# A two-layer streaming encoder step: first tokens scaled before their transpose, step weights loaded once, fixed places for long-lived tiles

## The chip, the cores and the metric

One core of a Trainium2 chip runs the whole step as one program. The metric is device time in microseconds (us), from the profiler's clock; lower is better. Engines: PE is TensorE (its weight loads are listed as PEld), DVE is VectorE, ACT is ScalarE, POOL is GpSimd, SP is SyncE, which here issues every DMA. Each engine takes its instructions in the order that was fixed when the program was built.

## What is computed

Two request groups go through the same weights: a prompt of 1024 tokens and a sample of 32 tokens with carried states. Layer 0 is a Mamba-2 SSD mixer, layer 1 an HGRN2 mixer, each followed by a SwiGLU FFN. The parts that the change touches are the first norm, the input projections of the SSD mixer and the step `dt`:

```python
def rmsnorm(x, w):
    y = x * rsqrt(mean(x * x, -1) + 1e-6)
    return y * w
# SSD mixer, on h = rmsnorm(x, ssd_norm_w)
proj = h @ in_w                       # 1024 -> 5152 = z 2048, xbc 3072, dt 32
xbc  = silu(causal_conv4(proj[xbc]))  # x 2048, B 512, C 512
dt   = softplus(proj[dt] + dt_bias)
y, S = ssd_scan(x, dt, -exp(A_log), B, C, S0)
out  = (rmsnorm_groups((y + D * x) * silu(z)) * gnorm_w) @ out_w
# every layer: x = x + out;  x = x + (silu(hn @ w_gate) * (hn @ w_up)) @ w_down
```

## The kernel before, in words

Tokens come in two halves: half 0 is prompt tokens 0 to 511, half 1 is prompt tokens 512 to 1023 with the 32 sample tokens behind them (`LEN` 512 and 544). All activations are kept transposed, features on the partitions and tokens along the free dimension; the residual is `acc[h][m]`, eight tiles of 128 features per half. Every product is made of three matmuls of rounded halves: high by high, high by low, low by high (`product`, lines 282 to 284); so each normalized activation tile `h`, `l` and each weight tile `wh`, `wl` is a pair, made by a ScalarE copy and a VectorE subtraction (`split`, `wsplit`).

The opening (lines 1167 to 1179 and 576 to 590) does this:

- `x_rows` loads 128 tokens as two row tiles of 512 columns; `load_x` transposes them on TensorE (line 161), squares them on ScalarE with a running sum (`xss`), and copies the transposed pieces into `acc` (line 168 and ScalarE in turn).
- `x_norm` takes 256 tokens: `x_rstd` makes the reciprocal root of each token on POOL (`xr`, one column a chunk), `over_partitions` spreads it over all partitions by `diag` and a product with ones (lines 181, 182), and `norm` makes, for each of eight feature tiles, `xf = acc * w * rstd` on VectorE (line 330), `h` on ScalarE and `l` on VectorE.
- `first_vectors`, `head_vectors` and `other_vectors` load small vectors. `head_vectors` loads `dcol` from `ssd_D` in two DMAs whose elements lie two apart in memory.
- `ssd_layer` first makes conv tile 16, the step (`ssd_dt`), conv tile 20, then `load_x` for all five chunks of half 1, the later vectors, and conv tiles 0 to 3. For these first conv tiles and for the step of half 0 the tokens go in two blocks of 256 columns; everything else of half 0 uses 512. `ssd_dt` loads its 32 weight columns four times side by side, so that the result stands on all four groups of 32 partitions.

Then the units of the SSD mixer follow: four z tiles, the chunks of the scan, the gate and the output product, with the next unit's conv tiles between; then the FFN, the HGRN2 mixer and its FFN. In the FFN, `ffn_unit` makes 256 columns of gate or up by a seven-product scheme from `unit_weights`; `unit_raw` takes its raw weights by a counter `NU`: odd units use the big `Y` tile, even ones two of the three `raw` tiles. Up and gate units alternate, and the down products of a group (`ffn_outs`, four loads into `raw`) run right after the next group's first gate unit.

Buffers are named by tags with a fixed count (`BUFS`): `x` 12, `n` 4, `s` 5, `xn` 16 for the normalized pairs, `raw` 3, `ws` 6. Places and the order of instructions on every queue come from a planner (`TileContext(nc, auto_bufs=True)`), which puts tiles into memory by their lifetimes and lets a tile wait for the one whose bytes it takes over; `high_priority` lifts the norm by 600 places.

Of the kernel before, what the change touches and what calls it, by code (L numbers as in the profile page):

```python
# [16 lines left out]
P = 128  # L17
# [13 lines left out]
NG = 4  # L31
# [11 lines left out]
BUFS = {"xn": 16, "x": 12, "ys": 8, "cb": 4, "xd": 2, "ec": 1, "ss": 1, "xr": 2, "n": 4, "w": 3, "s": 5}  # L43
WIDTH = {k: 512 if k == "xr" else TW if k in ("x", "w") else LEN[1] for k in BUFS}


@with_exitstack
def trunk_kernel(ctx, tc, x_prompt, x_sample, state_ssd, cache_conv, state_hgrn,
# [23 lines left out]
    def small(s, w=P, dt=F32):  # L72
        return sp.tile([P, w], dt, tag="s", bufs=BUFS["s"], name=nm(s))

# [41 lines left out]
    ident = cp.tile([P, P], F32, name="ident")  # L116
    make_identity(nc, ident)
    ones = cp.tile([P, P], F32, name="ones")
    V.memset(ones, 1.0)
    epsc = cp.tile([P, 1], F32, name="epsc")  # L120
    V.memset(epsc, EPS)
    lss = cp.tile([P, 13], F32, name="lss")
    epst = lss[:, 12:13]
    mhalf = cp.tile([P, 8], F32, name="mhalf")
    G.memset(mhalf, -0.5)
    cmask = cp.tile([P, P], F32, name="cmask")
# [4 lines left out]
    rmask = cp.tile([P, LEN[1]], F32, name="rmask")  # L131
# [4 lines left out]
    for i in range(2):  # L136
        t = cp.tile([P, P], F32, name=f"scz{i}")
        V.memset(t, 0.0)
        scz.append(t)


    acc = [[cp.tile([P, LEN[h]], F32, name=f"acc{h}_{m}") for m in range(KD)] for h in range(2)]

    xss = cp.tile([P, 2, 9], F32, name="xss")
    xr = cp.tile([P, 9], F32, name="xr")
# [38 lines left out]
    vc = cp.tile([P, NVC], F32, name="vc")  # L184
    cw = cp.tile([P, 96], F32, name="cw")
    cc = cp.tile([P, 72], F32, name="cc")
    dtb = cp.tile([P, 1], F32, name="dtb")
    acol = cp.tile([P, 1], F32, name="acol")
    dcol = cp.tile([P, 16], F32, name="dcol")
    lbt = cp.tile([P, 6, 8], F32, name="lbt")  # L190
# [29 lines left out]
    def other_vectors():  # L220
        rows = T("n", "rows")[:, :P]
        for c, src in ((C_FFN, ffn_norm_w), (C_HGN, hgrn_norm_w), (C_GN, ssd_gnorm_w),
                       (C_HG, hgrn_gnorm_w), (C_LB, hgrn_lower_bounds)):
            n = src.shape[0] * src.shape[1] // P
            dma(rows[c - NV0:c - NV0 + n, :], src.rearrange("o (m p) -> (o m) p", p=P))
        columns(rows, NVC - NV0, vc[:, NV0:])
        V.tensor_scalar_mul(vc[:, C_GN:C_HG + 1], vc[:, C_GN:C_HG + 1], 0.5)
        rows = T("n", "rows")[:, :P]
        dma(rows[:72, :], cache_conv.rearrange("o b k (m p) -> (o b k m) p", p=P))
        columns(rows, 72, cc)  # L230
# [29 lines left out]
    def wraw(parts, kt):  # L260
        raw = wp.tile([P, 1024], F32, tag="raw", bufs=3, name=nm("raw"))
# [6 lines left out]
    def wsplit(raw, kt):  # L268
        wh = wp.tile([P, 1024], F32R, tag="ws", bufs=6, name=nm("wh"))
        wl = wp.tile([P, 1024], F32R, tag="ws", bufs=6, name=nm("wl"))  # L270
# [51 lines left out]
    def norm(h, wc, out, tags, blocks=None, r=None):  # L322

        for (b0, bn) in blocks or ((0, LEN[h]),):
# [3 lines left out]
            for m in range(KD):  # L328
                xf = T("n", "xf")
                stt(xf[:, :bn], acc[h][m][:, b0:b0 + bn], vc[:, wc + m:wc + m + 1], r[:, :bn], MUL, MUL)  # L330
                if m == len(out):
                    out.append((T(tags[2 * m], "h", F32R), T(tags[2 * m + 1], "l", F32R)))
# [10 lines left out]
    carry = cp.tile([P, NCT, 3], F32, name="carry")  # L343
    newc = cp.tile([P, 2, 3, NCT], F32, name="newc")
    Sst = [cp.tile([P, 512], F32, tag="st", bufs=NG, name=f"Sst{g}") for g in range(NG)]
    cumd = [dp.tile([32, LEN[h]], F32, name=f"cumd{h}") for h in range(2)]
    ecumd = [dp.tile([32, LEN[h]], F32, name=f"ecumd{h}") for h in range(2)]
    lastd = [dp.tile([32, 5], F32, name=f"lastd{h}") for h in range(2)]

    @lifted("dt")  # L350
    def ssd_dt(h, xn, blocks):
# [3 lines left out]
        w = wload([(q * 32, (q + 1) * 32, ssd_in_w[0][:, 5120:5152]) for q in range(4)], KD, P)  # L355
# [30 lines left out]
        lastc = cp.tile([P, 5], F32, name=f"lastc{h}")  # L386
# [6 lines left out]
        elast = cp.tile([P, 32, 5], F32, tag="elast", bufs=2, name=f"elast{h}")  # L393
# [3 lines left out]
    def ssd_cols(h):  # L397
        pk, _, elast = dts[h]
        cols = cp.tile([P, 5, P], F32, tag="cols", bufs=1, name=f"cols{h}")
# [174 lines left out]
    def ssd_layer(after, w0):  # L574
# [10 lines left out]
        for c in range(5):  # L585
            load_x(1, c)
        other_vectors()
        lower_bounds()
        for t in ct[2:]:
            t()  # L590
        for i, (h, g) in enumerate(units):
# [16 lines left out]
            Yt = sp.tile([P, 4 * LEN[1]], F32, tag="Y", bufs=1, name=nm("Y"))  # L608
            u["Y"] = Yt.rearrange("p (j t) -> p j t", j=4)
            Ss = None  # L610
            if h:
                Ss = T("ss", "Ss")[:, :512]
                sr = T("xr", "sr")
# [35 lines left out]
    Shb = [cp.tile([P, 512], F32, tag="st", bufs=NG, name=f"Sh{i}") for i in range(2)]  # L649
# [137 lines left out]
    def hgrn_layer(after):  # L787
# [4 lines left out]
        for i, (h, e) in enumerate(units):  # L792
# [16 lines left out]
            if e % 2 == 0:  # L809
                yt = sp.tile([P, 4 * LEN[1]], F32R, tag="Y", bufs=1, name=nm("hy"))  # L810
# [62 lines left out]
    def unit_raw(src):  # L873

        NU[0] += 1
        if NU[0] % 2:
            t = sp.tile([P, 4 * LEN[1]], F32, tag="Y", bufs=1, name=nm("raw2"))
            halves = [t[:, q * 1024:(q + 1) * 1024] for q in range(2)]
        else:
            halves = [wp.tile([P, 1024], F32, tag="raw", bufs=3, name=nm("raw")) for _ in range(2)]  # L880
# [7 lines left out]
    def unit_weights(src):  # L888
# [3 lines left out]
        def hl(x):  # L892
            w = wp.tile([P, 1024], F32R, tag="ws", bufs=6, name=nm("wh"))
# [5 lines left out]
        s1 = T("xr", "s1")[:, :512].rearrange("p (k c) -> p k c", k=4)  # L899
# [202 lines left out]
    def mixer_ffn(mixer, layer, wc, nxt):  # L1102
# [10 lines left out]
        due = ffn_half(layer, 0, xn[0], tx[0], HEAD, lambda: r.append(x_stat(1, "ec")), [2])  # L1113
# [5 lines left out]
        due = ffn_half(layer, 1, xn[1], tx[1], 1, lambda: r.append(nxt and x_stat(0, "ss")),  # L1119
# [71 lines left out]
    for q in range(2):  # L1191
        wrow.append(T(("ec", "ss")[q], "wrow")[:, :512])
# [39 lines left out]
```

## Time and profile before

| | us |
|---|---|
| median of 3 runs | 2942.97 (2942.57 to 2947.24) |
| the profiled execution | 2942.06 |
| its span, first to last instruction | 2940.3 |
| TensorE busy | 2855.9 |
| VectorE busy | 2205.6 |
| ScalarE busy | 1551.3 |
| bytes moved by DMA | 283.42 MB, mean 96 GB/s |

How the views are read: a *window* row gives a stretch, its length, the busy us of PE, PEld, DVE, ACT and POOL with the number of instructions in brackets, the granted TensorE clock, the mean busy share of the DMA engines and GB/s. A *group* row gives line, engine, operation, out<-in by the program's names, shape and count, then busy us and mean ns of one, then the idle time of the engine just before them and what ended it. A *timeline* row gives the start, the us, the engine and line, the operation and how many of them were merged; in square brackets the idle time before it and who ended that. A *wait* row gives who waited for whom: us in total, times, longest. `SPq` is the DMA issue, `raw` a weight tile as loaded, `sc` and `mm` are PSUM tiles. Matmuls overlap, so the spacing of their starts says more than their length.

### The profile page before, as it was taken

Reading aid. Unit: us, or ns where it says so; the run is one execution under the profiler, and the core shown is the slowest. Engines: PE = TensorE matmul, PEld = TensorE weight load, DVE = VectorE, ACT = ScalarE, POOL = GpSimd, SP = SyncE. Lnnn points to the kernel's source line nnn. Section 1 sums busy time; section 2 is a strip of 40 time slices with the busy share of each in tenths; the row PEclk is TensorE's granted clock in tenths of the full one; section 3 lists DMA queues with packets and bytes.
Section 4 is the critical chain, followed back from the end, with each engine's and each line's share of the span. In section 5 each row is a group of like instructions: output and inputs, shape, how many; then the busy total and the mean of one; then the engine's idle time right before and its main releaser. Section 6 shows DMA issues by size and latency. Waiting matters only on the chain.

```text
span 2940.3 us, 49353 instructions
## 1 busy us (share of the span) xinstructions
PE 2855.9 (97%) x19655; PEld 2618.4 (89%) x19655; DVE 2205.6 (75%) x3879; ACT 1551.3 (53%) x2944; POOL 52.7 (2%) x156
## 2 busy tenths in 40 slices
PE   7999999999999999999999999999999999999998
PEld 6777788989988999899999888899988999999997
DVE  6877787877887987897777555655578977887777
ACT  6745545554643654455544555655554644454445
POOL 0000001000100000000000000000000000000000
PEclk9999999999999999999999999999999999999999
DMA  5443424343333333322333222222222333323332
GB/s 146 123 111 94 108 76 122 106 113 98 109 80 105 98 98 108 108 80 87 101 94 99 79 79 80 69 76 76 78 84 87 108 96 99 111 87 94 94 94 103
DMA packets 401346, 283.42 MB, mean 96 GB/s; under 512 B 28873, under 2 KB 386778, under 8 KB 401114
## 3 DMA queue, kind: packets, MB, share of 16 engines
q1 hardware_dynamic: 401114, 280.25, 32.7%
q8 instruction: 154, 2.52, 0.4%
q14 instruction: 78, 0.64, 0.1%
HBM read 272.39 MB, written 7.82 MB: 95 GB/s over the span
## 4 chain that ended last, share of the span: by engine, by line
PE 75%; DVE 12%; DMA 6%; ACT 5%; issue 2%; SPq 0%; DVEq 0%; POOL 0%; ACTq 0%; POOLq 0%
PE mm L282 16%; PE mm L284 16%; PE mm L283 16%; PE mm L919 3%; PE mm L917 3%; PE mm L918 3%; PE sc L919 3%; PE sc L917 3%; PE sc L918 3%; DMA cumB<-cumd 3%; DMA raw<-in_ffn_w_gate_dram 2%; DVE wh L89 2%; ACT wh L86 1%; PE sc L509 1%; ACT cumB L86 1%
## 5 line engine op out<-in xcount | busy, mean ns | idle before, releaser
L86 ACT ACTIVATE wh<-raw 128x512 fp32r<-128x512 f32 (+1 forms) x688 | 554.2, 817 | 592.4 <-PE mm L283 363.3
L282 PE MATMUL mm<-h,wh 128*128 128x272 f32 (+2 forms) x2064 | 675.0, 328 | 7.9 <-ACT h L86 3.9
L284 PE MATMUL mm<-h,wl 128*128 128x272 f32 (+2 forms) x2064 | 668.5, 324 | 2.7 <-DVE wl L89 2.7
L283 PE MATMUL mm<-l,wh 128*128 128x272 f32 (+2 forms) x2064 | 668.3, 324 | 1.3 <-DVE l L89 0.9
L89 DVE TENSOR_TENSOR wl<-raw,wh 128x1024 fp32r<-128x1024 f32 x308 | 376.0, 1222 | 150.7 <-ACT wh L86 149.3
L282 PEld LDWEIGHTS mm<-h,wh 128*128 128x128 f32 x2064 | 390.0, 189 | 38.1 <-ACT h L86 4.9
L284 PEld LDWEIGHTS mm<-h,wl 128*128 128x128 f32 x2064 | 390.2, 189 | 33.0 <-DVE wl L89 3.9
L283 PEld LDWEIGHTS mm<-l,wh 128*128 128x128 f32 x2064 | 390.4, 189 | 30.9 <-DVE l L89 3.1
L282 PE MATMUL mm<-fh,wh 128*128 128x272 f32 (+1 forms) x1056 | 343.2, 326 | 8.9 <-DVE fxd L89 7.8
L283 PE MATMUL mm<-fl,wh 128*128 128x272 f32 (+1 forms) x1056 | 342.2, 325 | 1.8 <-DVE fl L89 1.8
L89 DVE TENSOR_TENSOR acc<-mm,acc 128x272 f32<-128x272 f32 (+1 forms) x512 | 259.6, 524 | 110.3 <-PE mm L284 107.6
L284 PE MATMUL mm<-fh,wl 128*128 128x272 f32 (+1 forms) x1056 | 341.1, 324 | 0.6 <-DVE wl L89 0.6
L89 DVE TENSOR_TENSOR wh<-raw,wh 128x512 fp32r<-128x512 f32 x380 | 258.2, 688 | 20.6 <-ACT wh L86 17.7
L917 PE MATMUL mm<-th,wh 128*128 128x272 f32 (+1 forms) x912 | 260.9, 286 | 0.4 <-ACT s L86 0.4
L919 PE MATMUL mm<-th,wh 128*128 128x272 f32 (+1 forms) x912 | 259.6, 285 | 0.2 <-DVE wh L89 0.2
L918 PE MATMUL mm<-tl,wh 128*128 128x272 f32 (+1 forms) x912 | 259.6, 285 | 0.0
L282 PEld LDWEIGHTS mm<-fh,wh 128*128 128x128 f32 x1056 | 198.8, 189 | 26.9 <-DVE fxd L89 9.3
L283 PEld LDWEIGHTS mm<-fl,wh 128*128 128x128 f32 x1056 | 199.6, 189 | 17.7 <-DVE fl L89 3.4
L284 PEld LDWEIGHTS mm<-fh,wl 128*128 128x128 f32 x1056 | 199.5, 189 | 16.1 <-DVE wl L89 1.0
L917 PE MATMUL sc<-h,wh 128*128 128x272 f32 (+1 forms) x608 | 173.7, 286 | 0.5 <-ACT wh L86 0.5
L917 PEld LDWEIGHTS mm<-th,wh 128*128 128x128 f32 x912 | 171.7, 188 | 2.5 <-ACT s L86 1.7
L919 PE MATMUL sc<-h,wh 128*128 128x272 f32 (+1 forms) x608 | 173.3, 285 | 0.0
(261 smaller groups left out, 5961.0 us busy)
## 6 DMA issues: line engine op xcount, KB each, us to landing
raw<-in_ffn_w_down_dram SPq DMA_DIRECT2D x90, 512.0 KB, 3.5
raw<-in_ffn_w_gate_dram SPq DMA_DIRECT2D x88, 512.0 KB, 4.9
raw<-in_ffn_w_up_dram SPq DMA_DIRECT2D x88, 512.0 KB, 3.8
raw<-in_ssd_in_w_dram SPq DMA_DIRECT2D x80, 512.0 KB, 4.6
raw<-in_hgrn_in_w_dram SPq DMA_DIRECT2D x64, 512.0 KB, 4.1
cumB<-cumd SPq DMA_DIRECT2D x64, 256.0 KB, 4.1
raw<-in_ssd_out_w_dram SPq DMA_DIRECT2D x32, 512.0 KB, 3.7
raw<-in_hgrn_out_w_dram SPq DMA_DIRECT2D x16, 512.0 KB, 3.2
```

The costliest lines, as they stand in the source:

```text
L86: A.activation(out=out, in_=in_, func=f, **kw)
L89: (eng or V).tensor_tensor(out=out, in0=a, in1=b, op=op)
L282: PE.matmul(ps[:, :bn], a, mh, start=(k == 0), stop=False)
L283: PE.matmul(ps[:, :bn], a, ml, start=False, stop=False)
L284: PE.matmul(ps[:, :bn], b, mh, start=False, stop=(k == n - 1))
L509: PE.matmul(pp, Btok[:n, :], xw[:n, :], start=True, stop=True)
L917: PE.matmul(ps[:, :n], a, mh, start=(k == 0 and not more), stop=False, skip_group_check=True)
L918: PE.matmul(ps[:, :n], a, ml, start=False, stop=False, skip_group_check=True)
L919: PE.matmul(ps[:, :n], b, mh, start=False, stop=(k == 3), skip_group_check=True)
```

## The change

It has these parts:

- `first_norm` takes the place of `x_norm` for half 0. It scales the token rows by their own reciprocal root while tokens are on the partitions (four 128x512 scalings for 256 tokens), transposes the scaled rows (16 a call) into PSUM, and makes `h` and `l` straight from PSUM with the norm weight as a column scale. `load_x` still makes the residual. Half 1 keeps `x_norm`.
- `dt_weights` loads the 32 columns once and spreads them four times by a broadcast read in the split.
- `other_vectors` uses two row tiles of its own instead of two of the four `n` tiles.
- In `ssd_layer`, the chunks of half 1 are loaded one after each of conv tiles 0 to 3, the last after them, then the later vectors and the lower bounds.
- Long-lived tiles get fixed places in one tile `fixed` (`place`), the normalized pairs a fixed tile `xnt`; the small tiles of tag `s` become rings of their own (`rings`, `hec`), all other tags get one width. Scratch `s1`, the kept reciprocal roots and the final norm's rows move to the state tiles `st`. The counter `NU` is advanced after `unit_raw` instead of before.

The diff, cut to what is spoken of:

```diff
-BUFS = {"xn": 16, "x": 12, "ys": 8, "cb": 4, "xd": 2, "ec": 1, "ss": 1, "xr": 2, "n": 4, "w": 3, "s": 5}
-WIDTH = {k: 512 if k == "xr" else TW if k in ("x", "w") else LEN[1] for k in BUFS}
+FIXED = 14368
+BUFS = {"x": 12, "ys": 8, "cb": 4, "xd": 2, "ec": 1, "ss": 1, "xr": 2, "n": 4, "w": 3}
+WIDTH = {k: TW for k in BUFS}
...
-    def small(s, w=P, dt=F32):
-        return sp.tile([P, w], dt, tag="s", bufs=BUFS["s"], name=nm(s))
+    rings = {"diag": (0, 2), "cbm": (2, 2), "Btok": (4, 2), "hT": (0, 2), "hSp": (2, 4), "fss": (4, 2), "nco": (0, 1)}
+    at = {}
+
+    def small(s, w=P):
+
+        at[s] = at.get(s, -1) + 1
+        if s == "hec":
+            return hec[at[s] % 3][:, :w]
+        first, n = rings[s]
+        return smalls[first + at[s] % n][:, :w]
...
-    ident = cp.tile([P, P], F32, name="ident")
+    fixed = cp.tile([P, FIXED], F32, name="fixed")
+    used = [0]
+
+    def place(w):
+        used[0] += -(-w // 16) * 16
+        return fixed[:, used[0] - -(-w // 16) * 16:][:, :w]
...
     def other_vectors():
-        rows = T("n", "rows")[:, :P]
+        rows = sp.tile([P, P], F32, tag="rows", bufs=2, name=nm("rows"))
...
+    xnt = cp.tile([P, 16, LEN[1]], F32R, name="xn")
+    XN = [xnt[:, i] for i in range(16)]
...
+    @lifted("norm")
+    def first_norm(rows, out, c0):
+
+
+        x_rstd(P, c0, c0 + 2)
+        scaled = []
+        for c in (c0, c0 + 1):
+            for q in range(2):
+                t = T("n", "xs")[:, :512]
+                V.tensor_scalar_mul(t, rows[c][q], xr[:, c:c + 1])
+                scaled.append(t)
+        for m2 in range(4):
+            ps = psum_sc()
+            for j in range(4):
+                m = 2 * m2 + j // 2
+                PE.transpose(ps[:, j * P:(j + 1) * P],
+                             scaled[2 * (j % 2) + m // 4][:, (m % 4) * P:(m % 4 + 1) * P], ident)
+            for m in (2 * m2, 2 * m2 + 1):
+                if m == len(out):
+                    out.append((XN[2 * m], XN[2 * m + 1]))
+                xh, xl = [t[:, c0 * P:(c0 + 2) * P] for t in out[m]]
+                src, w = ps[:, (m % 2) * 256:(m % 2 + 1) * 256], vc[:, C_SSDN + m:C_SSDN + m + 1]
+                act(xh, src, AF.Copy, scale=w)
+                stt(xl, src, w, xh.bitcast(F32), MUL, SUB)
...
+    def dt_weights():
+
+        raw = wp.tile([P, 2 * TW], F32, tag="raw", bufs=3, name=nm("raw"))[:, :1024][:, :KD * 32]
+        raw = raw.rearrange("p (k c) -> p k c", k=KD)
+        dma(raw, ssd_in_w[0][:, 5120:5152].rearrange("(k p) c -> p k c", p=P))
+        four = raw.unsqueeze(2).to_broadcast([P, KD, 4, 32])
...
-        w = wload([(q * 32, (q + 1) * 32, ssd_in_w[0][:, 5120:5152]) for q in range(4)], KD, P)
+        w = dt_weights()
...
-        for c in range(5):
+        for c, t in enumerate(ct[2:]):
+            t()
             load_x(1, c)
+        load_x(1, 4)
         other_vectors()
         lower_bounds()
-        for t in ct[2:]:
-            t()
...
-        NU[0] += 1
         if NU[0] % 2:
-            t = sp.tile([P, 4 * LEN[1]], F32, tag="Y", bufs=1, name=nm("raw2"))
+            t = sp.tile([P, 4 * TW], F32, tag="Y", bufs=1, name=nm("raw2"))
...
-        s1 = T("xr", "s1")[:, :512].rearrange("p (k c) -> p k c", k=4)
+        NU[0] += 1
+        s1 = st[NU[0] % 2][:, :512].rearrange("p (k c) -> p k c", k=4)
...
-        x_norm(0, xns[0], q * 256, 256)
+        first_norm(rows, xns[0], 2 * q)
```

## Rows read from the trace of the kernel before

**Rows 1.** TensorE's line of section 1: busy us (share), instructions.

```profile
PE 2855.9 (97%) x19655; PEld 2618.4 (89%) x19655; DVE 2205.6 (75%) x3879; ACT 1551.3 (53%) x2944; POOL 52.7 (2%) x156
```

**Rows 2.** Busy time by stretch, the opening and a stretch of the middle.

```profile
0.00:80.00 80.00, 58.66 (x420) 54.44 (x421) 52.93 (x150) 50.75 (x132) 6.43 (x20) 0.96 0.52 134
...
1200.00:1800.00 600.00, 592.29 (x4029) 550.19 (x4028) 436.38 (x785) 307.67 (x541) 0.00 (x0) 1.00 0.30 91
```

**Rows 3.** Timeline of TensorE, pieces: start, us, operation, [idle before <-releaser].

```profile
10.71 4.78 PE L161 MATMUL mm<-ident,xrow 128*128 128x128 f32 x30
...
17.52 0.36 PE L282 MATMUL mm<-h,wh 128*128 128x256 f32 x1
...
41.82 0.28 PE L282 MATMUL mm<-h,wh 128*128 128x256 f32 x1
...
42.41 0.28 PE L284 MATMUL mm<-h,wl 128*128 128x256 f32 x1
45.84 0.38 PE L282 MATMUL mm<-h,wh 128*128 128x256 f32 x1 [3.15 <-DVE dt L95]
...
80.46 0.48 PE L282 MATMUL mm<-h,wh 128*128 128x512 f32 x1
```

**Rows 4.** Windows of the opening, columns as in rows 2.

```profile
17.50:42.70 25.20, 22.61 (x170) 20.47 (x169) 16.07 (x41) 11.28 (x30) 0.97 (x1) 1.00 0.31 76
42.70:80.70 38.00, 29.25 (x215) 27.90 (x216) 28.69 (x72) 28.48 (x72) 2.65 (x8) 0.91 0.53 134
...
20.00:35.00 15.00, 13.05 (x91) 11.31 (x92) 13.20 (x32) 8.79 (x22) 0.97 (x1) 1.00 0.05 0
```

**Rows 5.** PE's waits to 81 us: us, times, longest.

```profile
PE sc L195 <- DMA rows<-in_ssd_conv_b_dram: 4.8, 1, 4.8
```

**Rows 6.** Groups by shape, VectorE, 8 to 31 us: busy, mean ns.

```profile
L92 DVE SCALAR_TENSOR_TENSOR xf<-acc,vc,rstd 128x256 f32<-128x256 f32 x16 | 7.3, 482 | 0.0
L89 DVE TENSOR_TENSOR l<-xf,h 128x256 fp32r<-128x256 f32 x16 | 6.5, 423 | 0.2 <-ACT h L86 0.2
L181 DVE TENSOR_SCALAR diag<-ident,xr 128x128 f32<-128x128 f32 x4 | 1.1, 286 | 0.9 <-POOL xr L89 0.9
L89 DVE TENSOR_TENSOR wl<-raw,wh 128x1024 fp32r<-128x1024 f32 x3 | 3.7, 1223 | 0.3 <-ACT wh L86 0.3
```

**Rows 7.** Tile views of dcol, then of raw: time from issue to landing.

```profile
DMA to landing us min/median/max: 21.5/21.5/21.5
...
DMA to landing us min/median/max: 2.5/3.9/14.5
```

**Rows 8.** Timeline of SP, the issuing queue, 11 to 31 us.

```profile
11.20 4.06 SPq L98 DMA_DIRECT2D raw<-in_ssd_in_w_dram  x6
...
16.52 2.41 SPq L98 DMA_DIRECT2D dcol<-in_ssd_D_dram  x2
...
27.85 2.80 SPq L98 DMA_DIRECT2D raw<-in_ssd_in_w_dram  x1
```

**Rows 9.** Groups by shape, VectorE, 80 to 860 us, then to 81.

```profile
L92 DVE SCALAR_TENSOR_TENSOR z<-z,mm 128x272 f32<-128x272 f32 x32 | 13.9, 436 | 18.1 <-ACT z L86 18.1
...
L372 DVE TENSOR_SCALAR dt<-dt,acol 128x512 f32<-128x512 f32 x1 | 0.5, 481 | 0.0
```

**Rows 10.** ScalarE to 81 us: two groups by shape, then a timeline row.

```profile
L86 ACT ACTIVATE h<-xf 128x256 fp32r<-128x256 f32 x16 | 6.6, 416 | 2.7 <-DVE xf L92 2.3
...
L86 ACT ACTIVATE pre<-mm 128x256 f32<-128x256 f32 x8 | 2.7, 367 | 0.5 <-PE mm L284 0.5
...
42.41 1.06 ACT L86 ACTIVATE wh<-raw 128x1024 fp32r<-128x1024 f32 x1 [8.80 <-DMA raw<-in_ssd_in_w_dram]
```

**Rows 11.** Timeline of POOL: the reciprocal roots of the first tokens.

```profile
7.32 0.71 POOL L89 TENSOR_TENSOR xr<-xss,mhalf 128x2 f32<-128x2 f32 x1 [5.94 <-DVE xss L95]
...
15.26 1.00 POOL L89 TENSOR_TENSOR xr<-xss,mhalf 128x2 f32<-128x2 f32 x1 [2.38 <-DVE xss L95]
```

**Rows 12.** PE's waits, 860 us to the end: us, times, longest.

```profile
PE mm L282 <- DVE fxd L89: 7.8, 7, 2.1
```

More of the change, by code (lines that the diff above doesn't have):

```diff
@@ L130, in trunk_kernel @@
     umask = cmask.bitcast(U32)
-    rmask = cp.tile([P, LEN[1]], F32, name="rmask")
+    rmask = place(LEN[1])
     V.memset(rmask, 1.0)
@@ L136, in trunk_kernel @@
     for i in range(2):
-        t = cp.tile([P, P], F32, name=f"scz{i}")
+        t = place(P)
         V.memset(t, 0.0)
         scz.append(t)
-    acc = [[cp.tile([P, LEN[h]], F32, name=f"acc{h}_{m}") for m in range(KD)] for h in range(2)]
-    xss = cp.tile([P, 2, 9], F32, name="xss")
-    xr = cp.tile([P, 9], F32, name="xr")
+    acc = [[place(LEN[h]) for m in range(KD)] for h in range(2)]
+    xss = place(2 * 9).rearrange("p (a b) -> p a b", b=9)
+    xr = place(9)
     def x_rows(h, c):
@@ L182, in over_partitions @@
             PE.matmul(out[:, c * P:c * P + n], ones[:n, :], d[:n, :n], start=True, stop=True)
[L184 to L190, printed above, removed]
+    vc = place(NVC)
+    cw = place(96)
+    cc = place(72)
+    dtb = place(1)
+    acol = place(1)
+    dcol = place(16)
+    lbt = place(6 * 8).rearrange("p (a b) -> p a b", b=8)
     c1, c0, nc1 = lbt[:, 3, :], lbt[:, 4, :], lbt[:, 5, :]
@@ L260, in wraw @@
     def wraw(parts, kt):
-        raw = wp.tile([P, 1024], F32, tag="raw", bufs=3, name=nm("raw"))
+        raw = wp.tile([P, 2 * TW], F32, tag="raw", bufs=3, name=nm("raw"))[:, :1024]
         r3 = raw.rearrange("p (k c) -> p k c", k=kt)
@@ L340, in accumulate @@
         tt(d, ps[:, :bn], d, ADD)
-    carry = cp.tile([P, NCT, 3], F32, name="carry")
-    newc = cp.tile([P, 2, 3, NCT], F32, name="newc")
-    Sst = [cp.tile([P, 512], F32, tag="st", bufs=NG, name=f"Sst{g}") for g in range(NG)]
+    carry = place(NCT * 3).rearrange("p (a b) -> p a b", b=3)
+    newc = place(2 * 3 * NCT).rearrange("p (a b c) -> p a b c", b=3, c=NCT)
+    st = [place(TW) for _ in range(NG)]
+    Sst = [t[:, :512] for t in st]
     cumd = [dp.tile([32, LEN[h]], F32, name=f"cumd{h}") for h in range(2)]
@@ L385, in ssd_dt @@
         act(pk[96:128, :L], cum[96:128, :L], AF.Exp)
-        lastc = cp.tile([P, 5], F32, name=f"lastc{h}")
+        lastc = place(5)
         V.tensor_copy(lastc[96:128, :4], pk[96:128, P - 1:H1:P])
@@ L646, in half_two_dt @@
         dts[1] = ssd_dt(1, xns[1], BLK[1])
-    Shb = [cp.tile([P, 512], F32, tag="st", bufs=NG, name=f"Sh{i}") for i in range(2)]
+    Shb = [t[:, :512] for t in st[:2]]
     Sh = [Shb[e // 4][:, (e % 4) * P:(e % 4 + 1) * P] for e in range(8)]
@@ L873, in unit_raw @@
     def unit_raw(src):
-        NU[0] += 1
         if NU[0] % 2:
-            t = sp.tile([P, 4 * LEN[1]], F32, tag="Y", bufs=1, name=nm("raw2"))
+            t = sp.tile([P, 4 * TW], F32, tag="Y", bufs=1, name=nm("raw2"))
             halves = [t[:, q * 1024:(q + 1) * 1024] for q in range(2)]
         else:
-            halves = [wp.tile([P, 1024], F32, tag="raw", bufs=3, name=nm("raw")) for _ in range(2)]
+            halves = [wp.tile([P, 2 * TW], F32, tag="raw", bufs=3, name=nm("raw"))[:, :1024] for _ in range(2)]
         out = []
@@ L1118, in mixer_ffn @@
         r = []
[L1119 removed]
+        due = ffn_half(layer, 1, xn[1], tx[1], 1, lambda: r.append(nxt and x_stat(0, st[3])),
                        [2] if nxt else [1, 1])
```

52 lines of the change are left out of this document (31 added, 21 removed).

## The prediction

> **What bounds the kernel now.** I read the share of each engine first: TensorE is busy 97% of the span [rows 1]. So a part of this change is worth something only where TensorE stands still or is fed badly. Next, busy time by stretch [rows 2]: in 0 to 80 us TensorE is busy 58.7 of 80 us; from 1200 to 1800 592.3 of 600. The opening, up to the first z tile, loses some 21 us, nearly three times what those 600 us of the middle lose. The end of the opening is easy to see: the conv and step products of the first unit are 256 columns wide, and the first 512-wide product starts at 80.46 [rows 3].
>
> The opening by its pieces: a quarter (24 matmuls of 256 columns, half a token block of one weight tile) takes 24 x 0.118 = 2.83 us when nothing stops it (the five matmuls from 41.82 to 42.41 [rows 3]). Fourteen quarters are due: conv tiles 16, 20, 0 to 3, and the step. The first matmul starts at 17.52, seven quarters (170 matmuls in 17.5 to 42.7, of which 168 are theirs [rows 4]) are done at 42.7, then TensorE waits 3.15 us for the step's VectorE row, and the other seven with 40 token transposes take until 80.46 [rows 3, 4]. Its longest wait but that by releaser is a load at the start (4.8) [rows 5]; the rest is made of short ones and of matmuls that come slower than 0.118.
>
> Two causes stand behind this. First, until 31 us VectorE does the norm: 16 scalings `xf` (7.3 us), 16 low parts `l` (6.5), 4 `diag` (1.1), between the copies into the residual [rows 6]; the norm reads the residual, so the transposes and copies come before it. Second, the weight queue: two loads of 4 KB each for `dcol` are issued at 16.5, land after 21.5 us, and while they run a single weight issue takes 2.8 us where six took 4.06 [rows 7, 8]; from 20 to 35 us nothing is moved, 0 GB/s [rows 4]. The slowest weight load of the run takes 14.5 us against a median of 3.9 [rows 7]: it is the one issued at 27.85, since its split begins at 42.41, after ScalarE waited 8.8 us for it [rows 10]. What queues behind it on ScalarE and VectorE holds the step's row back.
>
> **The change, part by part.**
> **First tokens.** Removed: 16 `xf`, 16 `l`, 4 `diag`, two `rstd` copies and four 128-wide products over the diagonals. Added: 8 scalings of 128x512 by a column, 32 transposes, and 16 fused multiply-subtracts that read PSUM. On VectorE: a 512-wide scaling by a column is 0.481, so 3.8 us; the fused form from PSUM isn't there at 256 columns, the nearest is `z<-z,mm` at 272 with 0.436 (from SBUF `xf` took 0.482) [rows 6, 9], so 7.0 to 7.7. Sum: 14.9 removed, 10.8 to 11.5 added, 3.4 to 4.1 saved. ScalarE: 16 high parts at 0.416 from SBUF become 16 from PSUM, nearest `pre<-mm` at 0.367: 0.8 saved, and the two `rstd` [rows 10]. TensorE: 30 transposes took 4.78 us, so 32 cost 5.1 [rows 3]; the four diagonal products that go are worth less. Cover: TensorE waits for the norm anyway in those microseconds; without that cover it is 5 us at most.
>
> [...]
>
> More than the saving, the order changes: the squares come from the token rows, the reciprocal root is ready at 8.03 (7.32 + 0.71) [rows 11], and nothing then needs the residual. First half: 8.0 + 1.9 (4 scalings) + 3.5 (8 low parts) + 1.2 (VectorE's part of the first weights' split [rows 6]) = 14.6, so the first quarter ends near 15.3. In the kernel before its 24 matmuls start at 17.52 and are paced by VectorE; it ends about 22. Second half: its root was ready at 16.26 [rows 11]; I keep that, + 1.9 + 3.5 + 1.2 gives 22.9. Meanwhile the step's and conv 20's first quarters can run (15.3 + 5.7 = 21.0), then three second quarters end at 22.9 + 8.5 = 31.4, against 39.6 (42.41 less one quarter); the seventh at 34.2 instead of 42.5. Gain so far: 8 us.
>
> **Step weights once.** Four loads of 128 KB become one, for each half. Six weight issues took 4.06 us from 11.20 [rows 8]; three fewer save about 2 us of SP's time and of the wait for the weights behind them. In the first half this helps the step's quarter to run early, counted above; in the second half TensorE doesn't wait there: zero. The split has the same sizes.
>
> **Tokens of the second half.** Five chunks in one run become one after each conv tile, and the later vectors come after them. The 40 transposes, the squares and the copies are the same number. From 42.7 to 80.7 ScalarE is busy 28.5, VectorE 28.7, TensorE 29.3 of 38 us [rows 4]: three engines at three quarters each, taking turns. Spreading lets them overlap. Lower bound of that stretch: 29.3; upper: 38.0 as now. TensorE enters it at 34.2 in place of 42.5. End of the opening between 34.2 + 29.3 = 63.5 and 34.2 + 38.0 = 72.2. I take 68, between them, since ScalarE and VectorE serve their queues in order and the `dcol` loads remain. 80.5 - 68 = **12.5 us**.
>
> **Own buffers, fixed places.** The vectors' rows, the rings, the fixed normalized tokens, the states used as scratch: none adds an instruction. They change which reuse waits for which, and a scheduler that orders by readiness may reorder anything. TensorE idles 1.3% in 1200 to 1800 [rows 2], so there is little to win there, and a lost order costs what it idles more. The trace of before can't show it; I bound it by what TensorE idles in 1200 to 1800, 7.7 us, either way [rows 2], and take 0, since nothing in the edit favours a sign.
>
> Sum: the profiled execution took 2942.1 us (span 2940.3 and 1.8 around it); the median of the runs is 2943.0, within 1 us. 2942.1 - 12.5 = 2929.6, say **2930**.
>
> **Rivals.**
> *A. The weight queue decides.* `dcol` is untouched. Before, the weights of conv 0 were issued just ahead of it (last of the six, which end at 15.26, with `dcol` at 16.52 [rows 8]). If with fewer issues ahead `dcol` slips in front of them, they land when the queue frees, at 16.5 - 2 + 21.5 = 36 at the earliest, plus the split (1.06 on ScalarE, 1.2 on VectorE [rows 6, 10]): 4 us after TensorE wants them, and the other weights and tokens bunch behind. Then the stretch is no shorter than now: end 38 + 38 = 76, gain 4 to 5: **2938**. For it: three issues fewer, nothing that holds `dcol` back. Against: the order before. [...]
>
> *B. Slower: the weight ring in the FFN.* The counter now turns over after its test, so gate units take two of the three `raw` buffers and up units the big one, the reverse of now. The down-projection loads (four per group) come right after a gate unit; the next gate's two halves now queue behind them and are needed some three parts later instead of nine. A weight load lands in 3.9 us (median) [rows 7]. TensorE's FFN waits are short now: 7.8 us in 7, longest 2.1 [rows 12]. There are 21 groups (5 + 5 + 5 + 6). It decides once a group loses over 12.5 / 21 = 0.6 us; at 1.0 us it costs 21 and gives 2930 + 21 = **2951**; at 2.1, 2974. Against it: a down block keeps TensorE about 22 us (192 matmuls), and the slots come free during it.
>
> *C. Better than the sum.* The stretch packs to its lower bound (63.5, 17 us), or false reuse waits later go too (up to 8): **2922**.
>
> *D. It doesn't reach the end.* The residual copies, now without a taker, are put off and are paid later on VectorE and ScalarE; and the transposes cost their 5 us after all. What is left goes into waits of unit 0: within 0.2%, **2940**.
>
> **How the numbers follow.** Forecast 0.50, A 0.17, B 0.12, C 0.13, D 0.08. About 0.2%, 6 us, is what a measurement of this kernel can tell from no change. Faster by more than that: forecast, C, and a quarter of A (whose centre is 5 us): 0.67. Same: most of A, and D: 0.21. Slower: B, 0.12. The range runs from the better bound with a little of the later gain (2942 - 17 - 7 = 2918) to D with the 8 us of the reordering on top (2948).
>
> **What would show it.** Right: the first 256-wide conv matmul near 10 to 11 us, the seventh quarter done near 34, the first 512-wide product near 68, and busy TensorE in 0 to 80 us up by 10 or more while the later stretches stay. The 0 GB/s gap is still there, as long as before. A: the same gap, with a wait of ScalarE for a weight load before conv 0. B: the FFN stretches 1200 to 1800 and 2250 to 2860 longer, TensorE waiting on `wh` or `s`. D: the first 512-wide product early, but 80 to 200 us less busy. The forecast is wrong if the first conv matmul doesn't move: then the conv bias rows (the load that TensorE waits for until 9.16) or the squares hold it.

## The result, and the profile after

The changed kernel takes 2914.13 us (median of 4 runs, 2910.56 to 2915.18), the kernel before 2945.1 beside it: ratio 0.9891, 95% interval 0.9875 to 0.9907. The forecast was 2930 (2918 to 2948): faster, as said, but by about 30 us where 12.5 were expected, and the time lies below the range. The profiled execution has a span of 2911.8.

TensorE's share, the answer to [rows 1]:

```profile
PE 2848.0 (98%) x19679; PEld 2617.9 (90%) x19679; DVE 2205.2 (76%) x3867; ACT 1549.3 (53%) x2942; POOL 42.2 (1%) x156
```

Busy time by stretch, columns as in [rows 2]:

```profile
0.00:80.00 80.00, 56.37 (x416) 53.74 (x416) 49.65 (x116) 46.10 (x104) 4.37 (x21) 0.91 0.50 131
80.00:90.00 10.00, 0.00 (x0) 0.00 (x0) 0.00 (x0) 0.00 (x0) 0.00 (x0) 0.55 0.41 102
200.00:400.00 200.00, 200.00 (x992) 157.90 (x992) 156.31 (x227) 112.29 (x206) 7.41 (x25) 1.00 0.37 102
1200.00:1800.00 600.00, 597.68 (x4022) 554.51 (x4021) 437.18 (x784) 311.21 (x541) 0.00 (x0) 1.00 0.31 91
```

The opening, which was to gain, lost: 56.4 busy us in the first 80 against 58.7 [rows 2], and from 80 to 90 no engine does anything. The middle, which was to stay, gained: TensorE is busy 5.4 us more in 1200 to 1800 [rows 2], and in 200 to 400 it has no gap at all, where the kernel before had 8.9 us of them:

```profile
200.00:400.00 200.00, 191.08 (x939) 150.13 (x939) 149.51 (x217) 103.47 (x187) 8.66 (x25) 1.00 0.37 98
```

TensorE's timeline, the answer to [rows 3]; line 303 is the product, 182 the token transpose, 345 the transpose of `first_norm`:

```profile
9.99 2.56 PE L345 MATMUL sc<-fixed,xs 128*128 128x128 f32 x11
...
18.02 0.41 PE L345 MATMUL sc<-fixed,xs 128*128 128x128 f32 x2 [2.26 <-DVE xs L339]
...
23.28 0.56 PE L303 MATMUL mm<-xn,wh 128*128 128x256 f32 x1
...
64.54 1.12 PE L182 MATMUL sc<-fixed,xrow 128*128 128x128 f32 x4 [9.20 <-DMA xrow<-in_x_prompt_dram]
...
91.32 1.12 PE L182 MATMUL sc<-fixed,xrow 128*128 128x128 f32 x4 [13.70 <-DMA xrow<-in_x_prompt_dram]
...
93.37 0.78 PE L303 MATMUL mm<-xn,wh 128*128 128x512 f32 x1
```

The first 256-wide matmul comes at 23.28 (forecast 10 to 11, before 17.52), the first 512-wide one at 93.37 (forecast 68, before 80.46). Between them TensorE waits 9.20 and 13.70 us for token loads of half 1.

To place the rest I cut both executions at four matmuls that each kernel has: the first and last of the scan's output product (line 520 before, 583 after) and of the HGRN2 state product (752 and 815). All times in this table and its like below are starts of those matmuls in the profiled executions, subtracted:

| us | before | after | difference |
|---|---|---|---|
| start to first scan product | 107.6 | 123.9 | +16.3 |
| the scan (half 0 and 1) | 764.9 | 737.6 | -27.4 |
| to the first HGRN2 state product (FFN 0 mostly) | 774.5 | 767.9 | -6.6 |
| HGRN2 | 559.1 | 553.9 | -5.2 |
| to the end (FFN 1 mostly) | 734.2 | 728.5 | -5.7 |

So 44.9 us are gained behind the opening and 16.3 lost in it. Busy time in the scan, columns as in [rows 2], first before, then after:

```profile
107.60:872.50 764.90, 737.57 (x4914) 640.97 (x4915) 591.42 (x915) 412.04 (x834) 45.29 (x131) 1.00 0.38 104
123.90:861.40 737.50, 731.19 (x4914) 638.54 (x4913) 590.03 (x913) 411.40 (x834) 36.07 (x131) 1.00 0.39 106
```

TensorE stood still for 27.3 us of the scan before and for 6.3 after: 21.0 of the 27.4 us are idle time. The other 6.4 are shorter busy time; up to 3.4 of them, by my estimate, are the granted clock, which was at 0.50 for 6.8 us of the scan before and for none of it after, and the rest stays open. In the opening its idle time rose by 13.5 us (21.5 to 35.0), in HGRN2 it stayed (5.4 and 5.5).

### The profile page after: what moved, and what is told of

It is laid out like the page before. It is cut to its first block, busy times and chain, and to the rows that moved or that the text cites. A ratio compares the mean times of both kernels' runs of the same rounds, so it can differ in the third digit from the quotient of the medians.

```text
span 2911.8 us, 49126 instructions
## 1 busy us (share of the span) xinstructions
PE 2848.0 (98%) x19679; PEld 2617.9 (90%) x19679; DVE 2205.2 (76%) x3867; ACT 1549.3 (53%) x2942; POOL 42.2 (1%) x156
## 5 line engine op out<-in xcount | busy, mean ns | idle before, releaser
L303 PE MATMUL mm<-xn,wh 128*128 128x272 f32 (+2 forms) x1552 | 524.2, 338 | 0.0
L305 PE MATMUL mm<-xn,wl 128*128 128x272 f32 (+2 forms) x1552 | 519.2, 335 | 1.4 <-DVE wl L101 1.4
L304 PE MATMUL mm<-xn,wh 128*128 128x272 f32 (+2 forms) x1552 | 519.3, 335 | 0.0
L101 DVE TENSOR_TENSOR wl<-raw,wh 128x1024 fp32r<-128x1024 f32 x308 | 375.2, 1220 | 66.6 <-ACT wh L98 60.8
L101 DVE TENSOR_TENSOR fixed<-mm,fixed 128x272 f32<-128x272 f32 (+1 forms) x512 | 262.7, 524 | 184.1 <-PE mm L305 182.2
L305 PEld LDWEIGHTS mm<-xn,wl 128*128 128x128 f32 x1552 | 293.1, 189 | 31.0 <-issue 2.0
L303 PEld LDWEIGHTS mm<-xn,wh 128*128 128x128 f32 x1552 | 293.3, 189 | 29.6 <-issue 2.8
L304 PEld LDWEIGHTS mm<-xn,wh 128*128 128x128 f32 x1552 | 293.2, 189 | 27.5 <-issue 1.2
L979 PE MATMUL sc<-xn,wh 128*128 128x272 f32 (+1 forms) x608 | 173.2, 285 | 0.0
L981 PE MATMUL sc<-xn,wh 128*128 128x272 f32 (+1 forms) x608 | 172.8, 284 | 0.0
```

Of the source, the lines that this page charges most:

```text
L101: (eng or V).tensor_tensor(out=out, in0=a, in1=b, op=op)
L303: PE.matmul(ps[:, :bn], a, mh, start=(k == 0), stop=False)
L304: PE.matmul(ps[:, :bn], a, ml, start=False, stop=False)
L305: PE.matmul(ps[:, :bn], b, mh, start=False, stop=(k == n - 1))
L979: PE.matmul(ps[:, :n], a, mh, start=(k == 0 and not more), stop=False, skip_group_check=True)
L981: PE.matmul(ps[:, :n], b, mh, start=False, stop=(k == 3), skip_group_check=True)
```

## Experiments 1: which part carries what

**The memory changes alone.** `mem_only` is the changed kernel with the opening as before; the fixed places, rings, widths and the moved counter stay.

```diff
-        first_norm(rows, xns[0], 2 * q)
+        x_norm(0, xns[0], q * 256, 256)
...
-        w = dt_weights()
+        w = wload([(q * 32, (q + 1) * 32, ssd_in_w[0][:, 5120:5152]) for q in range(4)], KD, P)
...
-        rows = sp.tile([P, P], F32, tag="rows", bufs=2, name=nm("rows"))
+        rows = T("n", "rows")[:, :P]
```

and the token loads in one run, as in the next diff.

> The changed kernel with its opening as it was: first norm in feature layout, step weights in four loads, tokens of half 1 in one run, vectors in the shared row tiles; the fixed places, rings, widths and the moved counter stay. The changed kernel reached its first 512-wide product at 93.4 us, 13 later than before, and yet ended 31 earlier. Theory 1: the places and buffers made the gain after 125 us (some 44 us) and the opening parts lost 13: here about 2945 - 44 = 2901, first 512-wide product near 80. Theory 2: the new opening order made the later gain too: here about 2943.

Measured 2895.51 (2894.34 to 2897.25), 0.9831 (0.9815 to 0.9847). Stages 105.8, 738.1, 768.4, 553.8, 729.5: the whole later gain, and the opening of before (first 512-wide product at 78.8). Theory 1 holds. The memory parts, which the prediction put at 0, are worth some 50 us by the medians (2945.6 - 2895.5) and 44.8 by the two profiled executions.

**Tokens back in one run.**

```diff
-        for c, t in enumerate(ct[2:]):
-            t()
+        for c in range(5):
             load_x(1, c)
-        load_x(1, 4)
         other_vectors()
         lower_bounds()
+        for t in ct[2:]:
+            t()
```

> The changed kernel with the token loads of half 1 in one run ahead of conv tile 0 again, nothing else. Theory 1: the token loads stood in SP's queue behind the step's stores and the small-element load of elast, and TensorE waited 9.2 and 14.0 us for them; here both waits go, 2914 - 15 to 20 = about 2896, and the first 512-wide product comes near 72. Rival: the small-element loads only jam something else: 2910 to 2916.

Measured 2896.83 (2893.92 to 2898.28), 0.9834 (0.9818 to 0.9849); first 512-wide product at 78.6: the total is as expected, the product comes later than the 72 of theory 1. The interleaving alone costs 17.3 us (2914.1 - 2896.8). What `first_norm`, the step weights and the vectors bring together is 2896.8 - 2895.5, nothing that the runs can tell from zero.

**`first_norm` alone on the memory changes** (the first hunk of `mem_only` left out).

> The memory changes (2895.5 alone) with first_norm as the only part of the opening that is changed; step weights in four loads, vectors and token loads as before. By the prediction's steps first_norm gives 8 us or more: 2888 or less, first 512-wide product near 70. Theory K (the 32 extra transposes and the order cost what the earlier root gives): 2894-2900, first 512-wide product at 77-81. Rival L (it costs): 2902 or more.

Measured 2895.52 (2894.11 to 2896.84), 0.983 (0.9816 to 0.9845), product at 77.7: 0.0 against `mem_only`. Theory K holds in its figures. Its reason isn't shown: with `first_norm` the first 256-wide matmul comes later (24.0 against 18.8 in `mem_only`), and the product a microsecond earlier.

**The counter, taken back and done alone.**

```diff
+        NU[0] += 1
         if NU[0] % 2:
...
-        NU[0] += 1
         s1 = st[NU[0] % 2][:, :512].rearrange("p (k c) -> p k c", k=4)
```

> The changed kernel with the counter advanced ahead of its test again, so gate units take the big tile and up units two raw tiles. Theory F: swapping the buffers of gate and up made the FFN's gain (about 13 us of the 44): here about 2927. Rival: the counter does nothing: 2914, within 3.

> The kernel before with the counter advanced after its test, nothing else. Theory F: about 2932. Rival B of the prediction: slower, 2950 or more. Neither: 2943 to 2945.

Taken back: 2942.9 (2941.25 to 2949.16), 0.9995 (0.9985 to 1.0004); alone on the kernel before: 2937.6 (2932.02 to 2938.53), 0.9971 (0.9959 to 0.9983). Theory F had the sign of both and the size of neither (2927 and 2932). Rival B is refuted in its sign. ScalarE's waits for down weights in FFN 0 (930 to 1570 us), first before, then with the counter moved alone:

```profile
ACT wh L86 <- DMA raw<-in_ffn_w_down_dram: 69.4, 19, 5.0
```

```profile
ACT wh L86 <- DMA raw<-in_ffn_w_down_dram: 6.7, 6, 2.2
```

B saw that gate and up units swap buffers, and feared for the gate weights behind the down loads. It overlooked that before the swap it was the down loads that came late; with it they go out ahead of the gate loads. In the same stretch ScalarE and VectorE together wait 33.2 us for gate and up loads, where they waited 40.5, and the wait of [rows 12] falls from 7.8 us to 0.9 in this kernel. But the counter is worth 29 us in the changed kernel and 8 in the one before, and 17.4 of the 29 lie in the scan (737.6 against 755.0), which has no gate or up unit. That had to be another mechanism.

## Experiments 2: why the scan got faster

The scan's decay blocks `cumB` are loaded from DRAM, and ScalarE works on them first. ScalarE's waits from 130 to 850 us, first before, then after:

```profile
ACT cumB L86 <- DMA cumB<-cumd: 70.0, 32, 6.2
```

```profile
ACT cumB L98 <- DMA cumB<-cumd: 2.4, 6, 0.7
```

The issuing queue SP waits as well, for line 520, the product that reads `cumB`; in the changed kernel this wait doesn't occur. Before, 130 to 850 us:

```profile
SPq L98 <- PE sc L520: 84.3, 28, 6.1
```

Behind the standing ScalarE stand the copies and weight splits for TensorE, which waited 5.5 us for `wh` from ScalarE in the scan before and none after. From issue of a load to ScalarE's first use of its block the median is 4.4 us before and 9.9 after, while the load takes some 4 to 4.6 to land. The reason isn't the order: through the scan every engine's instructions stand in the same order with the counter either way. It is the place. The addresses in the built programs:

```
                        places used by     places whose last tile was a cumB
                        72 cumB blocks     (and how many blocks earlier)
before                  4                  68 (4 earlier)
after                   29                 8 (9 to 11 earlier)
after_counter_back      20                 48 (46 of them 4 earlier)
weight_width_back       4                  68 (4 earlier)
```

Before, a `cumB` block goes where the block two chunks earlier was, and its load is held until TensorE has used that one. With one width for all work tiles, and weight tiles of exactly twice that, the planner lays a `cumB` on whatever has long been free (`pre`, `yh`, `cth`, `raw`). Three runs test it.

**Four places of its own for `cumB`, everything else free to float.**

```diff
+    cbt = cp.tile([P, 4, TW], F32, name="cbt")
+    ncb = [0]
...
-            cb = T("cb", "cumB")[:, :512].rearrange("p (h t) -> p h t", t=P)
+            ncb[0] += 1
+            cb = cbt[:, ncb[0] % 4, :512].rearrange("p (h t) -> p h t", t=P)
```

> The changed kernel, but the decay blocks cumB of the scan get four places of their own, used in turn; every other tile stays as the changed kernel has it. Theory F (the scan's gain comes from cumB's loads: with one width for all tiles the planner puts each cumB block on bytes that have long been free, so its load is issued a chunk ahead, and ScalarE's wait for it, 70 us in 32 before, is gone): the wait comes back at 50 us or more, the time from the first to the last chunk of the scan grows from 737.5 to 755-765, total 2930-2942. Rival G (the gain comes from the other tiles that float, the weight tiles, ec, pre, xw, and cumB's wait is hidden anyway): the wait comes back, the stage stays at 738-742, total 2913-2919.

Measured 2931.23 (2930.0 to 2936.45), 0.9955 (0.994 to 0.997); scan 759.8, the other stages behind the opening within 2 us of the changed kernel. The wait, and the issuing queue in one chunk's length, first here, then in the changed kernel:

```profile
ACT cbt L98 <- DMA cbt<-cumd: 87.9, 40, 8.3
```

```profile
202.65 0.91 SPq L110 DMA_DIRECT2D cbt<-cumd  x2
203.72 0.40 SPq L110 DMA_DIRECT2D raw<-in_ssd_in_w_dram  x1
204.91 1.24 SPq L110 DMA_DIRECT2D ec<-ecumd  x2
213.14 0.92 SPq L110 DMA_DIRECT2D cbt<-cumd  x2
```

```profile
205.22 0.37 SPq L110 DMA_DIRECT2D raw<-in_ssd_in_w_dram  x1
206.43 1.25 SPq L110 DMA_DIRECT2D ec<-ecumd  x2
207.77 1.10 SPq L110 DMA_DIRECT2D cumB<-cumd  x2
214.53 0.37 SPq L110 DMA_DIRECT2D raw<-in_ssd_in_w_dram  x1
```

In the first the queue stands some 7 us ahead of each pair until the place is free; in the second the pair follows the loads ahead of it at once. Theory F holds: with this one wait 22 of the scan's 27 us come back. The sum of ScalarE's waits doesn't give the time, though: 87.9 us here at 759.8, 70.0 before at 764.9, 78.7 in `after_counter_back` at 755.0.

**Weight tiles 1024 wide again.**

```diff
-        raw = wp.tile([P, 2 * TW], F32, tag="raw", bufs=3, name=nm("raw"))[:, :1024]
+        raw = wp.tile([P, 1024], F32, tag="raw", bufs=3, name=nm("raw"))[:, :1024]
```

and the same for `wh` and `wl`.

> The changed kernel with the weight tiles (raw, wh, wl) 1024 wide again in place of 1104, that is 80 columns less in nine tiles, and nothing else. Theory F: 1104 is two of the other tiles' 552; at 1024 weight and work tiles no longer fit each other's places, cumB is back on four places, and the scan takes 755-765: total 2932-2945. Rival H (the width matters to nothing; the counter and the fixed places did it): 2912-2917.

Measured 2931.94 (2930.64 to 2934.12), 0.9955 (0.994 to 0.997), just below F's 2932; scan 759.5, ScalarE's wait 82.4 us. 80 columns fewer a weight tile undo most of the scan's gain. Rival H falls.

**Counter back, eight places for `cumB`** (the diff of the four places with 8, and the counter's).

> The changed kernel with the counter advanced before its test again (2942.9, first to last chunk 754.9, ScalarE waits 78.7 us for cumB's loads), and cumB in eight places of its own. Theory F: eight places let a load go two chunks ahead, the wait falls under 15 us, the scan takes 738-744 again, total 2925-2932, and the rest of the counter's 29 us, that of the two FFNs, stays lost. Rival G: the wait falls but the stage stays above 750, total 2938-2943.

Measured 2951.51 (2947.11 to 2954.61), 1.0023 (1.0013 to 1.0032). Neither theory: slower still, scan 761.2, wait 79.5 us. In the built program the planner uses eight places to put each load and ScalarE's work two chunks further ahead, so each load is again held until its place falls free just ahead of its use: the median from issue to use is 4.5 us. More places in turn don't help here; a place that is free long before its load's turn does. That the counter's 17.4 us in the scan go the way of the places rests on its row in the table and on ScalarE's wait there (78.7 us); this run, which was to bring them back, didn't.

**Rings, normalized pairs and `s1` back in pools**, the widths and the counter as changed.

```diff
-        if s == "hec":
-            return hec[at[s] % 3][:, :w]
-        first, n = rings[s]
-        return smalls[first + at[s] % n][:, :w]
+        return sp.tile([P, w], F32, tag="s", bufs=5, name=nm(s))
...
-    XN = [xnt[:, i] for i in range(16)]
+    XN = ["xn"] * 16
...
-        s1 = st[NU[0] % 2][:, :512].rearrange("p (k c) -> p k c", k=4)
+        s1 = T("xr", "s1")[:, :512].rearrange("p (k c) -> p k c", k=4)
```

> The changed kernel with the rings of small tiles, the normalized pairs and the scratch s1 back in pools; one width, the other fixed places and the moved counter stay, and cumB still lies on bytes long free. Theory F: these edits carry nothing of the 44 us: 2910-2918. Rival (they carry the rest, some 17 us, that the counter and cumB's places leave unexplained): 2920 or more.

Measured 2926.41 (2923.2 to 2927.37), 0.9925 (0.9902 to 0.9948): the rival's side, and my premise was wrong. The scan is 747.0, HGRN2 557.8. ScalarE waits 56.1 us for `cumB`. In this program 23 of the 72 `cumB` blocks lie partly on a `Btok`, a small tile that the chunk's last product has only just read. SP's waits from 130 to 850 us say the same, line 567 being that product:

```profile
SPq L106 <- PE sc L567: 162.6, 23, 15.3
```

So the small tiles' own places are a part of the gain too, by the same mechanism as far as the scan goes: they keep short-lived tiles out of the shared places. Which of the three edits does it wasn't taken apart. HGRN2's 4 us stay open; the granted clock is at 0.50 there for 6.8 us in this run and in the kernel before, and for 3.4 in the changed kernel, which can be a part of them and no more.

## Experiments 3: why the opening got slower

SP's timeline of the changed kernel, in pieces:

```profile
16.70 1.39 SPq L110 DMA_DIRECT2D fixed<-in_ssd_D_dram  x2
18.22 3.01 SPq L110 DMA_DIRECT2D sr<-in_state_ssd_dram  x1
21.33 24.40 SPq L110 DMA_DIRECT2D raw<-in_ssd_in_w_dram  x5
55.65 0.33 SPq L110 DMA_DIRECT2D ecumd<-dt  x1
...
58.69 1.00 SPq L110 DMA_DIRECT2D xrow<-in_x_prompt_dram  x2
...
69.00 1.57 SPq L110 DMA_DIRECT2D fixed<-lastd  x1
72.54 8.88 SPq L110 DMA_DIRECT2D raw<-in_ssd_in_w_dram  x1
81.47 6.93 SPq L110 DMA_DIRECT2D xrow<-in_x_prompt_dram  x4
```

Two things stand here. The first token load of half 1 comes behind the store `ecumd`, which SP holds for 9.8 us until ScalarE has made the step's row, at 55.65. And two loads of scattered elements jam the queue: `dcol` (`in_ssd_D`), after which five weight issues stretch over 24.40 us (21.8 of them in the issues themselves), and the step's last values (`fixed<-lastd`, 16-byte pieces to all partitions), after which one weight issue takes 8.88 and the tokens that TensorE needs at 77 are issued from 81.47.

**Rows loaded first.**

```diff
-            rows.append(T("x", "xrow")[:n, :512])
+            rows.append(T("xq" if h else "x", "xrow")[:n, :512])
...
+        rows1 = [x_rows(1, c) for c in range(5)]
         for c, t in enumerate(ct[2:]):
             t()
-            load_x(1, c)
-        load_x(1, 4)
+            load_x(1, c, rows1[c])
+        load_x(1, 4, rows1[4])
```

The ten row tiles `xq` have places of their own.

> The changed kernel with the ten row tiles of half 1 loaded ahead of conv tile 0, into places of their own; their transposes stay one chunk behind each conv tile. Theory Q (the interleaving costs 17 us because the token loads stand on SP behind the stores and loads of the step, which wait for ScalarE's row): TensorE's waits for xrow (23.4 us in 3) go, the first 512-wide product starts at 72-79 in place of 93.4, total 2890-2900. Rival O (transposes between conv tiles are a bad order by themselves): the product starts after 85, total 2905 or more.

Measured 2893.94 (2891.03 to 2895.89), 0.9824 (0.9804 to 0.9843); product at 70.8, no wait for `xrow` of half 1. Theory Q holds (the product a little earlier than its 72).

**The two loads made whole.**

```diff
-        dv = ssd_D.rearrange("o (j q) -> q (o j)", q=2)
+        dma(colt[:, :32], ssd_D.to_broadcast([P, 32]))
         for q in range(2):
-            dma(dcol[q * 64:(q + 1) * 64, :], dv[q:q + 1, :].to_broadcast([64, 16]))
+            V.tensor_copy(dcol[q * 64:(q + 1) * 64, :], colt[q * 64:(q + 1) * 64, q:32:2])
...
-    lastd = [dp.tile([32, 5], F32, name=f"lastd{h}") for h in range(2)]
+    lastd = [dp.tile([32, 4 + h], F32, name=f"lastd{h}") for h in range(2)]
...
-        elast = place(160).rearrange("p (h c) -> p h c", c=5)
+        elast = place(160)[:, :32 * nch].rearrange("p (h c) -> p h c", c=nch)
```

> The changed kernel with its two loads of scattered small elements made whole: ssd_D comes as rows of 32 to all partitions and VectorE makes dcol in two copies; the step's last values are stored without gaps, so that the load to all partitions has rows of 512 bytes in place of 16-byte pieces. Theory J (these two loads jam the queue, the 0 GB/s from 20 to 35 us and the raw and xrow issues of 5 to 9 us): the slow issues go, the first 512-wide product starts at 70-84 in place of 93.4, total 2893-2905. Rival Q (the token loads wait for the step's row, whatever the loads' form): 86 or later, total 2907-2914.

Measured 2892.46 (2891.85 to 2893.22), 0.9819 (0.9801 to 0.9838); product at 70.4. The same stretch of SP:

```profile
60.91 0.60 SPq L110 DMA_DIRECT2D fixed<-lastd  x1
64.17 0.38 SPq L110 DMA_DIRECT2D raw<-in_ssd_in_w_dram  x1
64.59 2.00 SPq L110 DMA_DIRECT2D xrow<-in_x_prompt_dram  x4
```

8.88 has become 0.38, the tokens are issued from 64.59, and TensorE's longest wait for them is 3.1 us. The five weight issues behind `dcol` take 3.5 us themselves in place of 21.8; they still stretch over 19.5, because SP then waits for VectorE between them (7.3 and 8.8 us). Theory J: the interleaving was bad because of the jam, and either edit mends it.

**Only `dcol` made whole.**

> The changed kernel with only dcol's load made whole, the step's last values in 16-byte pieces as they were. If dcol carries most of the 21.7 us that the two loads together gave: 2892-2899, the first 512-wide product at 70-78. If the second load does, which stands just ahead of the token loads: 2906-2912, product at 85 or later.

Measured 2905.58 (2903.53 to 2907.9), 0.9854 (0.9834 to 0.9873), product at 82.6, near the second of the two expectations: in this order `dcol` is worth 8.6 us, the second load the other 13.1, and the tokens' four-load issue still takes 6.25 us behind it.

**The same two edits on the kernel before.**

> The kernel before with the two loads made whole (dcol from whole rows by two VectorE copies, the step's last values without gaps), nothing of the change. Theory J by itself: the queue held the opening of the kernel before too, its first 512-wide product comes at 70-74 in place of 80.5, total 2934-2940. Rival (the engines hold it, as the prediction took it for the norm on VectorE): 78 or later, 2942-2946.

Measured 2936.51 (2931.51 to 2940.75), 0.9964 (0.9948 to 0.998); product at 73.6 in place of 80.5. So the queue held the opening of the kernel before as well: 7 us of its first 80, and some 10 of its whole time.

**Together, and with the old norm.** Tokens in one run with whole loads:

> Tokens of half 1 in one run (2896.8) with the two loads made whole as above. Theory J: the opening's first half is freed, first 512-wide product at 66-72 in place of 78.6, total 2884-2890. Rival (VectorE and ScalarE hold the opening, the queue was hidden): 76-79, total 2893-2898.

2890.46 (2889.91 to 2890.62), 0.9812 (0.9794 to 0.983), product at 72.5: just past theory J's 2890 and 72, and short of the rival's 2893 and 76. With whole loads the interleaving still costs 2 us (2892.5 against 2890.5), so the overlap that it was made for isn't to be seen. Rows first with whole loads, on the changed kernel:

> Rows loaded first and the two loads made whole, both edits on the changed kernel. If Q and J each hold for their own part: first 512-wide product at 60-70, total 2876-2888. If the ten token loads now hold back the weight loads behind them on SP: 76 or later, total 2892 or more.

2887.77 (2884.99 to 2891.2), 0.9807 (0.9783 to 0.9831), product at 66.6: the lowest median of all, though its runs overlap those of one run with whole loads, and at last the 68 that the prediction gave the opening. It with `x_norm`:

> Rows first and whole loads on the changed kernel (2887.8, first 512-wide product 66.6), with the old norm in place of first_norm. Theory N (with the queue free, VectorE's saving of some 3.5 us and the earlier root show): 2890-2895, product at 69-73. Rival K (first_norm is worth nothing at all, as in the runs with the queue jammed): 2886-2889.

2888.41 (2886.96 to 2889.47), 0.9795 (0.9776 to 0.9814), product at 68.1. Rival K holds: `first_norm` is worth nothing measurable even here.

## Why the prediction was wrong

- **Own buffers, fixed places** was the step that failed most: 0 within 7.7 us, measured 45 to 50 (`mem_only`). The bound was the wrong one. It took TensorE's idle time in 1200 to 1800 [rows 2] as that of the whole run, but 200 to 400 had 8.9 idle us in 200, and behind the opening TensorE idled 62.9 in all (84.4 of the span less 21.5), 27.3 of them in the scan. "The trace of before can't show it" was wrong too: the scan's wait of 70 us on ScalarE, and SP's of 84.3, stood in it to be read. "They change which reuse waits for which" was right; that list should have been made, one load with a short lead at a time.
- **First tokens.** The prices were right on VectorE: 8 scalings at 0.486 (forecast 0.481), 16 low parts from PSUM at 0.480 (0.436 to 0.482), where `xf` from SBUF took 0.482 [rows 6]. ScalarE's high parts took 0.479, not 0.367. Wrong was the step from VectorE's busy time to TensorE's start, "the first quarter ends near 15.3": TensorE's queue holds the transposes of the second 256 tokens ahead of the first conv matmul, which waits for the second root with them (18.02, 23.28). And nothing that it saved stood on the path: with the old norm the time is the same, whether `dcol` still jams the queue (2895.5 and 2895.5) or not (2888.4 and 2887.8).
- **Tokens of the second half.** "Upper: 38.0 as now" excluded a loss. The sum counted transposes, squares and copies, but not the five chunks' DMAs, which moved past the step's stores, its weight loads and the load of its last values on SP. Measured +17.3.
- **Step weights once.** 2 us of SP were forecast. `dcol` still went out at 16.70 (16.52 before [rows 8]), and the five weight issues behind it took 21.8. No run has this part alone; with `first_norm` and the vectors' tiles it brings nothing that can be told from zero (`tokens_one_run` against `mem_only`).
- **Rival A** had the right resource (0 GB/s, `dcol`, ScalarE waiting 7.2 us for a weight) and left the change a gain of 4 to 5 us for it, some 8 less than the forecast. `dcol` alone, whose elements lie two apart, measured 8.6; with the second scattered load, which no step named, it was 21.7, more than the whole forecast gain. The second load, in pieces of 16 bytes, cost the other 13.1, and both together some 10 in the kernel before.
- **Rival B** named the right ring with the wrong victim; the sign was the other. **C**'s "false reuse waits later go too (up to 8)" was the mechanism that won, some six times mis-sized.

The two large errors, 45 to 50 us too little for the memory parts and some 29 too much for the opening (12.5 gained against 16.3 lost), had opposite signs and hid each other by more than half. That the forecast of "faster" came true is luck: the part that was to bring it lost time.

## What to carry over

For each load of a steady loop read the time from issue to landing and to first use (for `cumB` before the change medians of 4.0 and 4.4 us); where the two are equal, ask which tile held the place before, since the planner's choice of place was worth more here than any instruction that the change saved. A DMA that moves in the program moves on its queue (the tokens of half 1 here, at +17.3 us): list what it now stands behind, and what that waits for. Look for loads of scattered elements on the queue, and make them whole (21.7 us here, 0.0 for `first_norm`), before tuning the work that waits behind them.

## What the hardware showed

The same weight load was issued in 0.38 us with whole loads (`whole_row_loads`) and, behind the scattered one, in 8.88 (the changed kernel). The granted TensorE clock falls within the opening: windows of the changed kernel,

```profile
14.70:18.00 3.30, 1.06 (x8) 0.83 (x9) 2.36 (x9) 3.11 (x11) 0.70 (x1) 1.00 0.37 85
18.00:23.20 5.20, 4.45 (x23) 3.49 (x24) 4.74 (x13) 3.02 (x9) 0.00 (x0) 0.66 0.05 0
23.20:26.50 3.30, 3.30 (x18) 3.30 (x17) 2.65 (x12) 2.20 (x9) 0.00 (x0) 0.50 0.05 0
26.50:35.00 8.50, 8.50 (x74) 8.50 (x74) 6.07 (x8) 4.30 (x8) 0.34 (x2) 1.00 0.05 0
```

TensorE is busy 1.06 of 3.30 us while it waits for `xs`; then the mean clock is 0.66 for 5.20 us, and from 23.2 to 26.5 it is at 0.50, though TensorE is then busy throughout: 18 matmuls in 3.30 us against 74 in 8.50 at 1.00. At the same rate as later those 18 would have taken 2.1 us, by my estimate. Over the first 95 us the mean granted clock is 0.86 in this kernel, 0.96 before, and 1.00 in `whole_row_loads` and `rows_first_whole_rows`, where TensorE waits for the tokens of half 1 for 3.9 us and for none (23.4 us in the changed kernel). How much of the opening's loss is waiting and how much the clock, no run separates.
